# The adaLN scale's products placed ahead of block 0, decay matrices in three wide products, one weight split moved to VectorE

## The chip, the cores and the metric

The kernel runs on one core of a Trainium2 chip. Its time is the device time of one execution in microseconds (us). TensorE (PE) multiplies matrices, VectorE (DVE), ScalarE (ACT) and GpSimd (POOL) work on vectors, and SyncE (SP) issues all the transfers of this kernel. Each engine takes its instructions strictly in the order in which the program was written, and waits where an operand isn't ready, so one late operand holds everything behind it on that engine.

## The reference, cut to what matters

One layer of a hybrid backbone: 1024 latent and 128 context tokens of width 1024 pass an adaptive layer norm, one wide projection, differential attention and a retention scan in both directions, gates, an output projection and a last layer norm. The change touches the modulation at the start, and the table of decays of the retention.

```python
mod = silu(cond) @ w_mod + b_mod
shift, scale, gate = split(mod, 3)
h = layernorm(x) * (1 + scale) + shift
proj = h @ w_in                    # qa, ka, va, za, qr, kr, vr, zr
...
log_g = log1p(-exp2(ret_decay))    # (2, 8): one per direction and head
decay_in = where(rel >= 0, exp(log_g * max(rel, 0)), 0)   # 128 x 128, each head and direction
inner = (q @ k.T) * decay_in       # in chunks of 128 tokens
```

## The kernel before

Tokens and context stand together as nine tiles of 128 rows (1152 columns once they are turned over). A float32 operand of the large products is split into a high part in the matrix engine's short float format (`whi`, of ACT) and the remainder (`wlo`), and each product is done as three: high by high, high by low, low by high. All engines' instructions are written out by one Python program, which carries a plan of its own: `Sched` (L40) keeps an estimated time for each engine, several generators ("streams") yield the time at which they can go on, and whichever is due next writes its instructions. So a change of an estimated cost moves later instructions too.

**First stage, `phase_h` (L385).** For each of the nine tiles of x, DVE and ACT normalise, PE turns over eight 128x128 squares into two banks of PSUM of the pool `tp` (which has two banks), and ACT copies them to `xnT`. In between, PE works out the scale of the modulation with the condition vector as the stationary operand: `scale_k(g, k)` is one product of block k of the condition with rows of the weights `wk`; the group g = 0 gives scale and shift of the blocks 0 and 1, g = 1 the scale of the blocks 2 and 3 (256 columns wide), g = 2 that of the blocks 4 to 7 (512 columns wide). `scale_cols(g)` has ACT copy the two resulting rows out of PSUM (`rows`), PE turn them into columns, and DVE add the bias into `m1` (printed `m`) and `sh`. The shift of the blocks 2 to 7 comes from DVE alone (`by_rows`, two row products a block; `junk` in the trace). `mod(j)` then makes block j of `Y`: an affine form `hf` of `xnT` (DVE for block 0, ACT for the others), the high part (ACT), the low part (DVE). As soon as a block is there, `k_part` adds its products to six running sums, three column chunks for each of two jobs (`qr` and `kr`, the list `first`): part 0 is high by high, part 1 takes the weights' low part, part 2 the low part of `Y`. The last two blocks are done in `last_parts`.

**The stages behind it, `phase_a` (L611).** A stream `dense` (L328) runs one projection after the other: k of head 0, then the first V job of the retention (`vr`, nine row tiles of 256 columns), q of head 0, k of head 1, the first V of attention, and so on. It loads two jobs ahead, and splits the weights of a job (`Job.split`, L292) just before it writes the products of the job ahead of it; the low parts are POOL's, except for the first job. The results go through two banks of PSUM (`dn`), so a chunk can start only when the chunk two before it has been read out: for q and k by DVE's shuffle into `sw` and its product into `rt` (rotary embedding, finished by POOL), for `vr` by a copy on ACT. Beside that stream `core` (the retention) runs, which begins with `decays` (L725): a chain of small operations on DVE up to `kdec`, and then for each of eight heads two exponentials on ACT (`ef`, `eb`) and three products on DVE, which make `DT`, the 128x128 decay matrix of that head. `ef` has two buffers there, and `eb` one.

Of the kernel before, what the change touches and what calls it, by code (L numbers as in the profile page):

```python
# [11 lines left out]
F32 = mybir.dt.float32  # L12
F32R = mybir.dt.float32r
AF = mybir.ActivationFunctionType
ALU = mybir.AluOpType
# [3 lines left out]
P = 128  # L19
D = 1024  # L20
KT = D // P
NL = 1024
NT = NL + P
NTILE = NT // P
NH = 8
CW = 384
# [113 lines left out]
def hybrid_step(ctx: ExitStack, tc: tile.TileContext, I: dict, O: dict):  # L140
# [14 lines left out]
    def act(out, in_, func=AF.Copy, after=None, **kw):  # L155
        nc.scalar.activation(out, in_, func, **kw)  # L156
        extra = sum(not isinstance(v, (int, float)) for v in kw.values())
        return sch.op("act", 0.06 + out.free_size() / 1200 + 0.09 * extra, after)
# [4 lines left out]
    def v_tt(out, a, b, op, after=None):  # L163
        nc.vector.tensor_tensor(out, a, b, op=op)  # L164
        return sch.op("dve", 0.07 + out.free_size() / 960, after, in_sbuf(a, b))
# [56 lines left out]
    pz = ctx.enter_context(tc.tile_pool(name="pz", bufs=1))  # L222
# [13 lines left out]
    def psum_now(tag):  # L236
        t, tok = psum(tag)
        tok[0] = 0.0
        return t
# [15 lines left out]
    class Job:  # L255
        def __init__(self, kind, srcs, rhs, evac, gate=None, pool2=None, pre=None, need=None):
            self.kind, self.srcs, self.rhs, self.evac = kind, srcs, rhs, evac
            self.gate, self.pool2, self.pre = gate, pool2, pre
            self.raw, self.hi, self.lo = [], [], []
            self.ready = 0.0  # L260
            self.need = need

        def load(self):
            for s in self.srcs:
# [60 lines left out]
    def dense(nxt, mark):  # L325


        cur = nxt()  # L328
        cur.load()
        yield 0  # L330
        cur.split("v")
        ahead = nxt()
        ahead.load()
        yield 0
        while cur is not None:
            if ahead is not None:
                ahead.split()
            after = nxt() if ahead is not None else None
            if after is not None:
                after.load()  # L340
            if cur.gate is not None:
                yield cur.gate
            yield from cur.run()
            cur, ahead = ahead, after
        done[mark] = True
# [16 lines left out]
    def phase_h(first, load_decays, decays_y):  # L362

        es = ExitStack()
        p0 = es.enter_context(tc.tile_pool(name="p0", bufs=1, reuse_waits="tile"))
        with es:
# [27 lines left out]
            GS = ((0, 4), (0, 2), (2, 6))  # L394
# [58 lines left out]
            def scale_k(g, k):  # L453

                n = (GS[g][1] - GS[g][0]) * P
                if k == 0:
                    scale_ps[g] = psum_now("tp" if g else "dn")
                mm(scale_ps[g][0:2, :n], sc[:, k, :], wm[g, k], k == 0, k == KT - 1)

            def scale_cols(g):  # L460

                n = GS[g][1] - GS[g][0]
                rows = p0.tile([2, 512], F32, tag="rows", name="rows")
                act(rows[:, :n * P], scale_ps[g][0:2, :n * P])
                tp = psum_now("tp")
                for j in range(n):
                    nc.tensor.transpose(tp[:, 2 * j:2 * j + 2], rows[:, j * P:(j + 1) * P], ident[0:2, 0:2])
                    sch.t += 0.107
                for j0, dst, a, m, one in (((0, m1, 0, 2, 1.0), (2, sh, 0, 2, 0.0)), ((0, m1, 2, 2, 1.0),),
                                           ((0, m1, 4, 4, 1.0),))[g]:  # L470
                    c0 = 8 + a if one else a
                    v_stt(dst[:, a:a + m, :], tp[:, 2 * j0:2 * (j0 + m)].rearrange("p (j r) -> p j r", r=2), one,
                          bm[:, c0:c0 + m].rearrange("p (j o) -> p j o", o=1).to_broadcast([P, m, 2]),
                          ALU.add, ALU.add)
# [15 lines left out]
            for i in range(NTILE):  # L490
                if i + 2 < NTILE:
                    stats(i + 2)
                if i + 1 < NTILE:
                    normalise(i + 1)
                for g in range(2):
                    tp = psum_now("tp")
                    for k in range(4):
                        kk = g * 4 + k
                        tpose(tp[:, k * P:(k + 1) * P], xt[i][:, kk * P:(kk + 1) * P])
                    act(xnT[:, g * 4:(g + 1) * 4, i * P:(i + 1) * P],  # L500
                        tp.rearrange("p (k c) -> p k c", k=4))
                for k in ((), (0, 1), (2,), (3,), (4,), (5,), (6, 7), (), ())[i]:
                    scale_k(0, k)
                if i >= 6:
                    (lambda: first[0].split_hi(), lambda: scale_cols(0), lambda: None)[i - 6]()
                if i == 7:
                    first[1].split_hi()
                if i == 2:
                    first[0].load()
                    first[1].load()  # L510
                    load_shift(2)
                    load_wk(1, 0)
                    load_wk(1, 4)
                    load_shift(3)
                    for k in range(0, KT, 2):
                        load_wk(2, k)
# [33 lines left out]
                    load_decays()  # L550

            mod(0)
            acc = [[psum_now(("dn", "dn", "a", "a", "a", "a")[3 * n + c]) for c in range(NC)] for n in range(2)]
            vw = [j.views() for j in first]

# [11 lines left out]
            for k in range(KT - 2):  # L567
                mod(k + 1)
                for part in range(3):
                    for n in range(2):  # L570
                        k_part(n, k, part)
                        if (k, part, n) in ((0, 1, 0), (2, 0, 1)):
                            scale_cols(1 + k // 2)
                    if part == 0 and k < 2:
                        for q in range(KT):
                            scale_k(k + 1, q)
                if k == 2:
                    next(stream)
            mod(KT - 1)
# [31 lines left out]
    def phase_a():  # L611
# [113 lines left out]
        def decays():  # L725
# [34 lines left out]
            yield act(kdec, kdec, AF.Exp) + 1.3  # L760
            v_ts(kdec, kdec, 0.125, None, ALU.mult)
            act(g128, lg[:, 24:32], AF.Exp, scale=float(P))
            for h in range(NH):
                ef = pz.tile([P, CW], F32, tag="tz", name="ef", bufs=2)
                eb = pa.tile([P, P], F32, tag="ust", name="eb")
                act(ef[:, :P], cst[:, 0, :], AF.Exp, scale=lg[:, h:h + 1])
                yield act(eb[:, :P], cst[:, 1, :], AF.Exp, scale=lg[:, 8 + h:9 + h])
                v_tt(ef[:, :P], ef[:, :P], cst[:, 2, :], ALU.mult)
                v_tt(eb[:, :P], eb[:, :P], cst[:, 3, :], ALU.mult)
                v_tt(DT[:, h, :], ef[:, :P], eb[:, :P], ALU.add)  # L770

        def cache():
            ts = {}
# [170 lines left out]
        jobs = []  # L944
# [12 lines left out]
            return f  # L957

        jobs[-1].evac = last_evac
        todo.extend(jobs)  # L960
        dma(rc, I["rope_c"])
        dma(rsn, I["rope_s"])
# [698 lines left out]
```

## Time and profile before

| | |
|---|---|
| median of three timed runs | 1690.24 us (1687.55, 1690.24, 1691.09) |
| the profiled execution's own time | 1692.03 us |
| its span, first to last instruction | 1690.2 us |
| mean granted clock of TensorE | 0.994 |
| bytes moved | 237.36 MB, mean 140 GB/s |

The kernel is read as a line of TensorE work with gaps in it. In a row of the timeline the first column is the start in us, the second the length of the group, then engine, line, operation, written operand <- read operands, shapes and count; in square brackets stands how long the engine had been idle before it, and what ended that wait. Most operations are written by helpers, so a line number says little: L149 is every product, L153 every transpose, L156 every operation of ACT, L164 and L185 the two-operand products of DVE and POOL, L169 and L173 DVE's operations with scalars. In a table of windows PEclk is the clock that TensorE was granted in that stretch, as a share of full speed.

### The profile page before, as it was taken

The page shows a single profiled execution, that of the slowest core. Times are in us where ns is not written, and L with a number is a line of the kernel's source. Part 1 is how long each engine was busy: PE and PEld are TensorE (multiplying, and loading weights), DVE is VectorE, ACT ScalarE, POOL GpSimd, SP SyncE. Part 2 cuts the span into 40 slices and gives each one's busy share as a digit, 9 for nine tenths or more (in the row PEclk, how much of TensorE's full clock was granted, in tenths as well). Part 3 has the DMA queues.
Part 4 walks back from the last instruction along what each step waited for, and adds up shares of the span by engine and source line. Part 5 has one row for each costly group of instructions (what it writes and reads, how often), then busy time and mean ns, then how long its engine had stood idle before and what let it go on. Part 6 is the DMA issues. An engine that isn't in the chain of part 4 may idle for free.

```text
span 1690.2 us, 27057 instructions
## 1 busy us (share of the span) xinstructions
PE 1657.3 (98%) x10515; PEld 1610.2 (95%) x10515; DVE 853.6 (51%) x1679; ACT 606.1 (36%) x1136; POOL 784.4 (46%) x546
## 2 busy tenths in 40 slices
PE   7999999999999999999999999999999999999998
PEld 4799999999999999999999999999999999999886
DVE  7736407314605536656565666566656033134666
ACT  5532222221221245455455555545555220012200
POOL 2246227334725657654757475757655321112200
PEclk9999999999999999999999999999999999999999
DMA  8254303421321383534434343525252577854532
GB/s 332 94 149 127 123 27 114 128 93 45 104 102 44 125 267 111 189 106 133 139 116 146 113 155 110 162 92 168 74 160 87 208 263 262 264 180 131 159 125 87
DMA packets 135697, 237.36 MB, mean 140 GB/s; under 512 B 15801, under 2 KB 103313, under 8 KB 134545
## 3 DMA queue, kind: packets, MB, share of 16 engines
q1 hardware_dynamic: 135568, 235.63, 43.3%
q8 instruction: 83, 1.36, 0.3%
q14 instruction: 46, 0.37, 0.1%
HBM read 161.08 MB, written 74.49 MB: 139 GB/s over the span
## 4 chain that ended last, share of the span: by engine, by line
PE 89%; DVE 3%; issue 2%; ACT 2%; DMA 1%; POOL 1%; SPq 0%; DVEq 0%; POOLq 0%; ACTq 0%
PE dn L149 59%; PE S L149 8%; PE o L149 6%; PE e L149 6%; PE a L149 5%; PE tp L153 5%; PE tp L149 1%; ACT E L156 1%; DMA xt<-in_x 1%; DMA ORd<-goh 0%; DVE eps L173 0%; DVE r L173 0%; DVE E L173 0%; ACT whi L156 0%; DVE nm L1097 0%
## 5 line engine op out<-in xcount | busy, mean ns | idle before, releaser
L149 PE MATMUL dn<-Y,whi 128*128 128x384 f32 x3200 | 829.7, 340 | 3.3 <-DVE rt L164 2.2
L149 PEld LDWEIGHTS dn<-Y,whi 128*128 128x128 f32 x3200 | 567.4, 189 | 4.9 <-DVE rt L164 2.5
L149 PE MATMUL dn<-Y,wlo 128*128 128x384 f32 x1600 | 535.6, 336 | 0.0
L185 POOL TENSOR_TENSOR wlo<-raw,whi 128x1024 fp32r<-128x1024 f32 x85 | 204.7, 2412 | 412.5 <-ACT whi L156 403.1
L149 PEld LDWEIGHTS dn<-Y,wlo 128*128 128x128 f32 x1600 | 300.5, 188 | 1.4 <-issue 0.9
L1097 DVE TENSOR_REDUCE nm<-S 128x1 f32<-128x1152 f32 x144 | 178.1, 1237 | 174.2 <-PE S L149 173.9
L189 POOL TENSOR_SCALAR E<-E,r 128x640 f32<-128x640 f32 x64 | 143.6, 2243 | 127.5 <-DVE r L173 87.0
L156 ACT ACTIVATE E<-S,nm 128x1152 f32<-128x1152 f32 x144 | 162.3, 1127 | 79.4 <-DVE nm L1097 74.5
L149 PE MATMUL dn<-whi,Y 128*128 128x256 f32 x864 | 158.9, 284 | 2.4 <-ACT vr L156 1.9
L149 PEld LDWEIGHTS dn<-whi,Y 128*128 128x128 f32 x864 | 135.4, 191 | 2.8 <-ACT vr L156 2.1
L149 PE MATMUL o<-wTh,V 128*128 128x256 f32 x576 | 133.5, 290 | 0.0
L156 ACT ACTIVATE wTh<-tp 128x512 fp32r<-128x512 f32 (+1 forms) x168 | 88.6, 543 | 112.9 <-PE tp L153 109.2
L156 ACT ACTIVATE whi<-raw 128x1024 fp32r<-128x1024 f32 x88 | 92.2, 1054 | 91.2 <-PE dn L149 85.0
L149 PE MATMUL dn<-wlo,Y 128*128 128x256 f32 x432 | 122.1, 283 | 0.0
L164 DVE TENSOR_TENSOR wTl<-tp,wTh 128x512 fp32r<-128x512 f32 (+1 forms) x168 | 99.6, 612 | 24.0 <-ACT wTh L156 24.0
L185 POOL TENSOR_TENSOR E<-E 128x640 f32<-128x640 f32 x64 | 100.4, 1569 | 5.3
L149 PE MATMUL S<-K,QH 128*128 128x384 f32 (+1 forms) x400 | 94.4, 339 | 6.2 <-ACT E L156 6.2
L149 PEld LDWEIGHTS o<-wTh,V 128*128 128x128 f32 x576 | 99.4, 188 | 0.2
L149 PE MATMUL S<-K,QL 128*128 128x384 f32 (+1 forms) x400 | 92.6, 335 | 0.0
L173 DVE SCALAR_TENSOR_TENSOR gt<-gt,dn 128x384 f32<-128x384 f32 x48 | 26.6, 554 | 120.2 <-DMA gt<-Gd 59.6
L153 PE MATMUL tp<-ident,E 128*128 128x128 f32 x584 | 86.8, 272 | 0.0
L169 DVE TENSOR_SCALAR KD<-tp,kdec 128x256 f32<-128x256 f32 (+1 forms) x48 | 16.0, 407 | 138.1 <-PE tp L153 138.1
(203 smaller groups left out, 2476.5 us busy)
## 6 DMA issues: line engine op xcount, KB each, us to landing
K<-Kd SPq DMA_DIRECT2D x8, 1280.0 KB, 8.3
Gd<-gt SPq DMA_DIRECT2D x48, 192.0 KB, 2.5
V<-Vd SPq DMA_DIRECT2D x24, 384.0 KB, 4.9
gt<-Gd SPq DMA_DIRECT2D x48, 192.0 KB, 2.5
Y<-OAd SPq DMA_DIRECT2D x16, 576.0 KB, 3.9
raw<-in_w_gate SPq DMA_DIRECT2D x16, 512.0 KB, 3.6
QH<-Qh SPq DMA_DIRECT2D x64, 128.0 KB, 3.0
QL<-Ql SPq DMA_DIRECT2D x64, 128.0 KB, 2.8
```

The lines of the kernel that those rows point to most:

```text
L149: nc.tensor.matmul(out, lhsT=lhsT, rhs=rhs, start=start, stop=stop)
L153: nc.tensor.transpose(out, in_, ident)
L156: nc.scalar.activation(out, in_, func, **kw)
L164: nc.vector.tensor_tensor(out, a, b, op=op)
L169: nc.vector.tensor_scalar(out, a, s1, s2, op0=op0, **kw)
L173: nc.vector.scalar_tensor_tensor(out, a, s, b, op0=op0, op1=op1, **kw)
L185: nc.gpsimd.tensor_tensor(out, a, b, op=op)
L189: nc.gpsimd.tensor_scalar(out, a, s1, None, op0=op0)
L1097: nc.vector.tensor_reduce(nm[:, m:m + 1], ps[:, :nb, :kw], axis=AX.XY, op=ALU.max, negate=True)
```

## The change

There are three edits. The scale's group 1 is no longer written after the first products of block 0: its first four products stand between the turning of tile 8 and block 0, the other four after block 0's part 0, and the copy of its rows follows at once; group 2 keeps its place after block 1's part 0, but the copy of its rows is written there instead of at the transposes. The copy of the rows is a function of its own, `scale_rows`; for group 0 it moves up by one tile, and the splitting of the first job's weights (`whi`) moves down by one tile for that. In `decays` the exponentials of the eight heads go into two tiles of 128x1024 each, and DVE makes all eight matrices in three products. The low parts of the first `vr` job are given to DVE.

```diff
@@ Job.__init__ / dense
             self.need = need
+            self.low = "p"
...
-                ahead.split()
+                ahead.split(ahead.low)
@@ phase_h
+            rows_of = {}
+
+            def scale_rows(g):
+                n = GS[g][1] - GS[g][0]
+                rows_of[g] = p0.tile([2, 512], F32, tag="rows", name="rows")
+                act(rows_of[g][:, :n * P], scale_ps[g][0:2, :n * P])
+
             def scale_cols(g):
                 n = GS[g][1] - GS[g][0]
-                rows = p0.tile([2, 512], F32, tag="rows", name="rows")
-                act(rows[:, :n * P], scale_ps[g][0:2, :n * P])
+                rows = rows_of[g]
...
-                if i >= 6:
-                    (lambda: first[0].split_hi(), lambda: scale_cols(0), lambda: None)[i - 6]()
+                if i == 6:
+                    scale_rows(0)
                 if i == 7:
+                    first[0].split_hi()
+                    scale_cols(0)
                     first[1].split_hi()
...
             mod(0)
+            for q in range(4):
+                scale_k(1, q)
...
                         k_part(n, k, part)
-                        if (k, part, n) in ((0, 1, 0), (2, 0, 1)):
+                        if (k, part, n) == (0, 0, 1):
+                            for q in range(4, KT):
+                                scale_k(1, q)
+                            scale_rows(1)
+                        if (k, part, n) in ((0, 1, 1), (2, 0, 1)):
                             scale_cols(1 + k // 2)
-                    if part == 0 and k < 2:
+                    if (k, part) == (1, 0):
                         for q in range(KT):
-                            scale_k(k + 1, q)
+                            scale_k(2, q)
+                        scale_rows(2)
@@ decays
+            ef = pa.tile([P, NH, P], F32, tag="SS", name="ef")
+            eb = pa.tile([P, NL], F32, tag="QD", name="eb").rearrange("p (h i) -> p h i", i=P)
             for h in range(NH):
-                ef = pz.tile([P, CW], F32, tag="tz", name="ef", bufs=2)
-                eb = pa.tile([P, P], F32, tag="ust", name="eb")
-                act(ef[:, :P], cst[:, 0, :], AF.Exp, scale=lg[:, h:h + 1])
-                yield act(eb[:, :P], cst[:, 1, :], AF.Exp, scale=lg[:, 8 + h:9 + h])
-                v_tt(ef[:, :P], ef[:, :P], cst[:, 2, :], ALU.mult)
-                v_tt(eb[:, :P], eb[:, :P], cst[:, 3, :], ALU.mult)
-                v_tt(DT[:, h, :], ef[:, :P], eb[:, :P], ALU.add)
+                act(ef[:, h, :], cst[:, 0, :], AF.Exp, scale=lg[:, h:h + 1])
+                f = act(eb[:, h, :], cst[:, 1, :], AF.Exp, scale=lg[:, 8 + h:9 + h])
+                yield f
+            v_tt(ef, ef, cst[:, 2:3, :].to_broadcast([P, NH, P]), ALU.mult)
+            yield v_tt(eb, eb, cst[:, 3:4, :].to_broadcast([P, NH, P]), ALU.mult)
+            yield v_tt(DT, ef, eb, ALU.add)
@@ phase_a
+        jobs[0].low = "v"
```

On TensorE, at the end of the first stage's transposes (tile 8 is the row with `raw`, `tp<-wk,sc` is group 1, `dn<-Y` and `a<-Y` are the running sums), the order moves like this:

```order
 L153 MATMUL tp<-ident,raw 128x128 x8
+L149 MATMUL tp<-wk,sc 2x256 x4
 L149 MATMUL dn<-Y,whi 128x384 x2
 L149 MATMUL a<-Y,whi 128x384 x4
-L149 MATMUL tp<-wk,sc 2x256 x8
+L149 MATMUL tp<-wk,sc 2x256 x4
 L149 MATMUL dn<-Y,wlo 128x384 x2
-L149 MATMUL a<-Y,wlo 128x384
-L467 MATMUL tp<-ident,rows 128x2 x2
-L149 MATMUL a<-Y,wlo 128x384 x3
+L149 MATMUL a<-Y,wlo 128x384 x4
+L474 MATMUL tp<-ident,rows 128x2 x2
```

Half of group 1 now stands ahead of block 0's first product, and the two transposes of its rows stand behind all six products of part 1.

On ScalarE, at the same place (the first four copies are those of the tiles 5 and 6, then come tile 7, tile 8 and the three pieces of block 0's high part):

```order
 L156 ACTIVATE xnT<-tp 128x4x128 x4
-L156 ACTIVATE whi<-raw 128x1024
+L156 ACTIVATE rows<-dn 2x512
 L156 ACTIVATE xnT<-tp 128x4x128 x2
-L156 ACTIVATE rows<-dn 2x512
-L156 ACTIVATE whi<-raw 128x1024
+L156 ACTIVATE whi<-raw 128x1024 x2
 L156 ACTIVATE xnT<-tp 128x4x128 x2
 L156 ACTIVATE Y<-hf 128x384 x3
```

The copy of group 0's rows and the first high split have changed places. Further down on ScalarE the copy of group 2's rows moves from behind block 3's pieces to ahead of them.

On VectorE, in the stage behind it (`kdec` ends the chain of small operations; the shuffle into `sw` and the product into `rt` read out the first chunk of k of head 0):

```order
 L164 TENSOR_TENSOR kdec<-kx,lg 128x16
-L666 STREAM_SHUFFLE sw<-dn 128x384
+L164 TENSOR_TENSOR wlo<-raw,whi 128x1024 x2
+L682 STREAM_SHUFFLE sw<-dn 128x384
 L164 TENSOR_TENSOR rt<-dn,rc 128x384
```

The two low splits of `vr`, which were the first work of POOL after its two memsets, now stand between `kdec` and that shuffle. The three wide products stand behind the shuffle and product of k's last chunk, where the 24 products of 128x128 stood, and the next work of DVE after them is the shuffle of q's first chunk, in both orders. ScalarE's exponentials keep their place, but the copy of the last chunk's context part (`rt<-dn 128x128`) stands behind two pairs of them and one high part of k (`qkh`), where it stood ahead of all pairs. Beyond this, the planner puts the retention's work of head 0 some products later into the stream of projections; from the retention of head 1 on the order of all engines is that of before.

## The prediction

> **What bounds the kernel now.** I read the page first, then TensorE's timeline for its gaps, the windows for its clock, and at each gap the timelines of the engines that it waited for.
>
> ```profile
> PE 1657.3 (98%) x10515; PEld 1610.2 (95%) x10515; DVE 853.6 (51%) x1679; ACT 606.1 (36%) x1136; POOL 784.4 (46%) x546
> ```
>
> TensorE is busy for 1657 of 1690.2 us. The edits neither add nor remove a product, so only TensorE's gaps, and the time in which it ran at a lower clock, can be won. Two stretches of a lower clock stand in the stages that the change touches; these are windows of 2 us, the last of 20 (length, then busy time of PE, weight load, DVE, ACT, POOL; then the granted clock, DMA share, GB/s):
>
> ```profile
> 32.00:34.00 2.00, 1.46 (x5) 1.13 (x4) 2.00 (x3) 1.87 (x3) 0.00 (x0) 0.69 1.07 394
> 34.00:36.00 2.00, 2.00 (x7) 0.53 (x6) 1.97 (x4) 1.34 (x2) 0.00 (x0) 0.50 0.60 230
> 36.00:38.00 2.00, 2.00 (x11) 0.76 (x10) 1.96 (x4) 0.00 (x0) 0.00 (x0) 0.96 0.05 18
> ...
> 92.00:94.00 2.00, 0.38 (x3) 0.38 (x4) 1.67 (x6) 0.98 (x4) 0.38 (x1) 1.00 0.00 0
> 94.00:96.00 2.00, 2.00 (x13) 2.00 (x12) 1.64 (x4) 2.00 (x6) 1.00 (x1) 0.55 0.05 12
> 96.00:98.00 2.00, 2.00 (x13) 2.00 (x13) 1.58 (x7) 0.97 (x4) 0.00 (x0) 0.60 0.96 210
> ...
> 100.00:120.00 20.00, 20.00 (x158) 20.00 (x157) 1.04 (x5) 5.60 (x10) 4.78 (x2) 1.00 0.52 128
> ```
>
> If the clock is either full or half, 0.55 and 0.60 make (0.45 + 0.40) x 2 / 0.5 = 3.4 us of half clock, which loses 1.7 us of work, right behind a gap of TensorE at 92 to 94. The first three rows hold 1.2 + 2.0 + 0.2, the same 3.4 us, also behind gaps.
>
> **Part 1, the first stage.** Here is TensorE from tile 8 to the products of group 2, and ACT beside it:
>
> ```profile
> 29.07 1.11 PE L153 MATMUL tp<-ident,raw 128*128 128x128 f32 x8
> 31.31 0.85 PE L149 MATMUL dn<-Y,whi 128*128 128x384 f32 x2 [1.13 <-ACT Y L156]
> 32.71 1.64 PE L149 MATMUL a<-Y,whi 128*128 128x384 f32 x4 [0.55 <-ACT Y L156]
> 34.28 4.53 PE L149 MATMUL tp<-wk,sc 128*2 128x256 f32 x16
> 38.74 0.62 PE L149 MATMUL dn<-Y,wlo 128*128 128x384 f32 x2
> ...
> 42.49 7.03 PE L149 MATMUL tp<-wk,sc 128*2 128x512 f32 x16
> ```
>
> ```profile
> 25.24 1.05 ACT L156 ACTIVATE whi<-raw 128x1024 fp32r<-128x1024 f32 x1
> 27.14 1.09 ACT L156 ACTIVATE xnT<-tp 128x512 f32<-128x512 f32 x2 [0.85 <-PE tp L153]
> 28.11 0.57 ACT L156 ACTIVATE rows<-dn 2x512 f32<-2x512 f32 x1
> ...
> 29.76 1.09 ACT L156 ACTIVATE xnT<-tp 128x512 f32<-128x512 f32 x2
> 30.73 0.94 ACT L156 ACTIVATE Y<-hf 128x384 fp32r<-128x384 f32 x2
> 32.13 0.52 ACT L156 ACTIVATE Y<-hf 128x384 fp32r<-128x384 f32 x1 [0.46 <-DVE hf L169]
> ```
>
> TensorE waits 1.13 + 0.55 us for block 0's high part. In ACT's new order the rows' copy (0.5) goes into the idle 0.85 ahead of 27.14, and both splits (1.0 each) follow tile 7 at 28.1. Tile 8's copies then run from 30.1 to 31.1 instead of 29.76 to 30.85, and the three high pieces from 31.1 to 32.5: DVE has `hf` ready earlier, as group 0's rows are copied ahead of 27.14 instead of at 28.11, so ACT's wait of 0.46 goes. The last piece ends at 32.5 against 32.65.
>
> TensorE can't start group 1 at once: both banks of `tp` hold tile 8, and the first is free when half of its copies are done, at 30.6. From there, four products. A product of group 2 (512 columns) counts as two in the trace, at 7.03 / 16 = 0.44 us each and full clock, so one of 256 columns takes 2 x 0.22, and four take 1.8. That gives 30.65 + 1.8 = 32.5, when block 0 is ready. A product of 384 columns takes 0.17 (two last 0.51 with the 0.34 of one, in rows below), so six of block 0 bring it to 33.55, four more of group 1 35.35. From the end of group 1 to the start of group 2 the trace has 42.49 - 38.74 = 3.75 us, which stays: **group 2 starts at 39.1 instead of 42.49, 3.4 us earlier.** Of these, 1.7 are the half clock. If the clock drops again, 1.7 are left. The gap that remains reaches from tile 8's last transpose (28.2, when tile 7 is copied, and 1.1 for the eight: 29.3) to 30.65, 1.3 us; before there were 1.13 and 0.55. Less idle time at that place speaks for the full clock.
>
> What hid group 1 before was nothing; what could come last now is the chain behind group 2, as its rows' copy stands ahead of block 3 on ACT:
>
> ```profile
> 49.55 0.59 ACT L156 ACTIVATE rows<-tp 2x512 f32<-2x512 f32 x1 [2.81 <-PE tp L149]
> 53.21 0.17 DVE L173 SCALAR_TENSOR_TENSOR m<-tp,bm 128x8 f32<-128x8 f32 x1 [3.86 <-PE tp L467]
> 64.34 0.21 ACT L156 ACTIVATE dec<-dec 128x32 f32<-128x32 f32 x1
> 64.47 1.36 DVE L164 TENSOR_TENSOR Y<-hf,Y 128x1152 fp32r<-128x1152 f32 x1 [1.40 <-ACT Y L156]
> 67.26 0.51 PE L149 MATMUL dn<-Y,whi 128*128 128x384 f32 x2
> ```
>
> From `m` to `dec` ACT makes four blocks in 11.0 us, 2.73 each. Block 7's low part ends at 65.83 and is used at 67.26: 1.43 us to spare. In the new order (on the old clock of TensorE, group 2 ending at 49.55) come rows 0.5, block 3 in 2.73, its low part 1.36, and then `m`: 54.3 instead of 53.2. That eats 1.1 of the 1.43, so 0.3 is left; I cost it at nothing. Without that cover it costs up to 1.1. Weights and shift loads come no later: the DMA share falls to 0.60 and then 0.05 in the windows above, so group 2's weights had landed by 36, and the next shift loads wait for group 1's buffers, which come free earlier.
>
> **Part 2, k of head 0 and the low parts of vr.**
>
> ```profile
> 69.84 1.23 DVE L164 TENSOR_TENSOR wlo<-raw,whi 128x1024 fp32r<-128x1024 f32 x1 [0.19 <-ACT whi L156]
> 74.63 4.78 POOL L185 TENSOR_TENSOR wlo<-raw,whi 128x1024 fp32r<-128x1024 f32 x2 [9.12 <-DVE tmp L169]
> 74.82 2.27 DVE L169 TENSOR_SCALAR tmp<-tmp 128x32 f32<-128x32 f32 x1
> 77.12 2.33 DVE L164 TENSOR_TENSOR tmp<-tmp 128x32 f32<-128x32 f32 x1
> 79.49 0.18 DVE L169 TENSOR_SCALAR tmp<-tmp 128x32 f32<-128x32 f32 x1
> 81.01 0.54 DVE L164 TENSOR_TENSOR rt<-dn,rc 128x384 f32<-128x384 f32 x1
> 79.05 0.34 PE L149 MATMUL dn<-Y,wlo 128*128 128x384 f32 x1
> 81.61 0.62 PE L149 MATMUL dn<-Y,whi 128*128 128x384 f32 x2 [2.22 <-DVE rt L164]
> ```
>
> Two operations of DVE on 128x32, whose like take 0.18 us, last 2.27 and 2.33, and each ends with one of POOL's two low splits (half way, at 77.0, and at 79.4). The whole chain, and behind it the first shuffle and `rt`, is late by 4.2 us, and TensorE has no free bank: 2.4 us lost (81.61 against 79.05 + 0.17). With both splits on DVE (two at a pitch of 1.15, out of the 1.23 of the first row: 2.3 us, right behind the chain) `rt` ends at 81.55 - 4.2 + 2.3 = 79.65, and TensorE goes on at 79.7, 0.5 us late instead of 2.4. **Gain 1.9 us**, bounded by 2.4 above and by -2.3 below (the splits add and the chain doesn't shrink). I take a value near the upper end, as POOL's ends and DVE's agree within 0.1 us, and POOL has nothing else queued in that stretch until the first rotary product.
>
> **Part 3, the decay matrices.**
>
> ```profile
> 85.91 0.28 PE L149 MATMUL dn<-whi,Y 128*128 128x256 f32 x1
> 88.97 2.41 POOL L185 TENSOR_TENSOR wlo<-raw,whi 128x1024 fp32r<-128x1024 f32 x1 [0.34 <-ACT whi L156]
> 89.31 2.22 DVE L164 TENSOR_TENSOR ef<-ef,cst 128x128 f32<-128x128 f32 x1 [1.47 <-ACT ef L156]
> 92.90 0.40 ACT L156 ACTIVATE eb<-cst,lg 128x128 f32<-128x128 f32 x1 [2.62 <-DVE DT L164]
> 93.62 0.39 PE L149 MATMUL dn<-whi,Y 128*128 128x256 f32 x1 [1.85 <-ACT vr L156]
> 112.59 0.38 ACT L156 ACTIVATE vr<-dn 128x256 f32<-128x256 f32 x1 [1.53 <-PE dn L149]
> 115.45 0.38 ACT L156 ACTIVATE vr<-dn 128x256 f32<-128x256 f32 x1 [2.48 <-PE dn L149]
> ```
>
> DVE's first `ef` product again lasts as long as POOL's split. ACT's second `eb` waits 2.62 us for the only buffer, and `vr`'s copy behind it keeps TensorE waiting. One tile of `vr` takes 2.86 us (115.45 - 112.59), nine take 25.7; from 85.91 to 115.4 are 29.5. **The 3.75 us too many are the gain**: 2.0 of the gap and 1.7 of half clock behind it. With two wide tiles no exponential waits for DVE. The three products (about 1.2 us each by the split's row, 3.7 in all, up to 7.4 if POOL's work collides) stand before DVE's next duty, the shuffle of q, which comes after the whole of `vr`; nobody waits. Wherever the cover of `vr` is gone, they would cost those 3.7.
>
> **The sum.** 3.4 + 1.9 + 3.75 = 9.05 us. Against the profiled execution: 1692.03 - 9.05 = **1683.0 us**. The median before is 1.8 below that execution, and the runs spread over 3.5, about two half-clock stretches. I read this as executions in which one such stretch fell out, and don't take the 1.8 off again; the low end of the range does. What lies behind (the retention of head 0 moved within the stream, SP's loads of its state moved past two stores of q) I cost at nothing: TensorE is busy for all of 100 to 120 us, with the planner's same rules behind it, and the order is the old one again after that.
>
> **Rivals.**
>
> [...] *The half clock is chance.* If a stall of 1.85 us doesn't set it, and where it falls is luck of each execution, only 9.05 - 2 x 1.7 = 5.65 is won: 1686.4. For it: the spread of the runs. Against it: both stretches begin right behind a gap. [...]
>
> *One cover fails.* The remaining gap of 1.3 us draws the half clock again, or ACT's chain behind group 2 ends last: 1.7 or up to 1.1 less, at most 1684.7.
>
> *DVE's chain isn't slowed by POOL.* Then the splits only add 2.3 us ahead of the first shuffle: 3.4 + 3.75 - 2.3 = 4.85, 1687.2. Against it: the matching ends.
>
> *Slower: ACT's queue.* The copy of the last chunk's context part stands behind two pairs of exponentials and a `qkh` that waits for POOL. Its bank is needed after the first tile of `vr`, 85.91 - 1.9 + 2.86 = 86.9; DVE's part of it (a shuffle and a product, together 1 us behind 84.0) ends at about 85.0, and the copy itself takes 0.3, so there are 1.6 us to spare. Beyond them every us of waiting (for POOL, or for the tile `cst`) is one of TensorE, with 1.7 for the clock. To lose all the gain and 3.4 us more, ACT must stand 12.4 us; a hold of 15 gives 1692.03 - 9.05 + 13.4 + 1.7 = 1698.1. Nothing in the trace holds it that long.
>
> *It doesn't do what it says*: the gain comes back as new gaps in the retention of head 0, whose work moved: about 1690.
>
> **How the numbers follow.** Forecast 0.48; one cover fails 0.22; clock by chance 0.14; chain not slowed 0.08; slower 0.04; given back 0.04. What a measurement can tell from no change is about 0.2%, 3.4 us, so faster means below 1686.9: 0.48 + 0.22 + 0.14 = 0.84. Within it: 0.08 + 0.04 = 0.12. Slower: 0.04. The range takes in the first three: up to 1686.6, and down by the 1.8 and the two small gaps that I left (1.3 and 0.5): 1679.4.
>
> **What would show it.** Right: the row of 16 products of 512 columns starts near 39, no window under 0.9 in 30 to 40 us or around 85 to 95, no gap over 0.5 before the third chunk of k, `vr` copies 2.86 apart from the first to the last, and DVE's small operations all near 0.2. Wrong: a clock under 0.7 near 33, a row of block 7's products that waits for DVE's `Y`, or a `vr` product that waits for ACT.

## The result, and the profile after

| | before | after |
|---|---|---|
| median of four timed runs | 1690.02 us (1687.55 to 1691.09) | 1680.66 us (1679.17 to 1683.20) |
| the profiled execution's own time, and its span | 1692.03, 1690.2 us | 1680.30, 1678.5 us |
| TensorE's mean granted clock | 0.994 | 0.998 |

The ratio of the medians is 0.9948, with a 95% interval of 0.9931 to 0.9965: faster by 0.5%, and 1680.66 lies 2.3 us below the forecast, inside its range. The two profiled executions are 11.7 us apart, the medians 9.4. From the page of the changed kernel, the busy time of the engines:

```profile
PE 1652.8 (98%) x10515; PEld 1606.1 (96%) x10515; DVE 846.0 (50%) x1660; ACT 605.7 (36%) x1136; POOL 780.1 (46%) x544
```

TensorE has the same 10515 products and 4.5 us less busy time, although none was taken away. The row counts how long products took, and at half clock they take longer: in the run with seven gaps (below) the products of 128x256 follow each other after 0.21 us at half clock and 0.12 at full. The changed kernel has three stretches of half clock fewer (counted below), and one costs 1.4 to 1.6 us where the runs below single it out, so the clock accounts for about all of the 4.5 us. The rest of the 11.7 us is idle time of TensorE that is gone.

**First stage.** TensorE in the changed kernel from tile 8 (`raw`) to group 2, then ACT beside it, in the timeline's columns:

```profile
28.00 1.09 PE L153 MATMUL tp<-ident,raw 128*128 128x128 f32 x8
30.37 1.89 PE L149 MATMUL tp<-wk,sc 128*2 128x256 f32 x8 [1.28 <-ACT xnT L156]
32.19 0.62 PE L149 MATMUL dn<-Y,whi 128*128 128x384 f32 x2
...
33.43 1.89 PE L149 MATMUL tp<-wk,sc 128*2 128x256 f32 x8
...
39.02 7.03 PE L149 MATMUL tp<-wk,sc 128*2 128x512 f32 x16
```

```profile
27.83 2.00 ACT L156 ACTIVATE whi<-raw 128x1024 fp32r<-128x1024 f32 x2
29.72 1.08 ACT L156 ACTIVATE xnT<-tp 128x512 f32<-128x512 f32 x2
30.68 1.36 ACT L156 ACTIVATE Y<-hf 128x384 fp32r<-128x384 f32 x3
```

One gap of 1.28 us is left where there were 1.13 and 0.55; it ends when half of tile 8's copies are done, which stand behind the two splits on ACT. Group 1 takes 1.89 + 1.89 us instead of 4.53, because the clock stays full (granted 1.00 in all windows of 2 us from 30 to 38, where before had 0.50 from 34 to 36). Group 2 starts at 39.02 instead of 42.49. About 0.4 us of that is the execution's start: TensorE waited 3.5 us for its first operand, and before 4.0, and a tile that neither kernel treats differently is turned over at 20.28 instead of 20.71.

**k of head 0 and `vr`.** DVE from the end of the small chain to the first chunk's read-out, and TensorE beside it:

```profile
71.35 0.18 DVE L169 TENSOR_SCALAR tmp<-tmp 128x32 f32<-128x32 f32 x1
...
72.74 2.36 DVE L164 TENSOR_TENSOR wlo<-raw,whi 128x1024 fp32r<-128x1024 f32 x2
...
75.64 0.54 DVE L164 TENSOR_TENSOR rt<-dn,rc 128x384 f32<-128x384 f32 x1
```

```profile
75.59 0.34 PE L149 MATMUL dn<-Y,wlo 128*128 128x384 f32 x1
76.23 0.62 PE L149 MATMUL dn<-Y,whi 128*128 128x384 f32 x2 [0.30 <-DVE rt L164]
...
80.50 0.28 PE L149 MATMUL dn<-whi,Y 128*128 128x256 f32 x1
```

Every small operation takes 0.2 us now, the two splits 2.36, and TensorE waits 0.30 us (0.47 between the end of the work and the next start) where it waited 2.22. In windows of 40 us (PE's busy time is the first number, the granted clock the third from the end), two of before and two of after:

```profile
0.00:40.00 40.00, 31.48 (x153) 18.75 (x154) 28.01 (x56) 23.67 (x37) 9.44 (x24) 0.96 0.89 330
...
80.00:120.00 40.00, 36.54 (x268) 36.34 (x269) 14.99 (x42) 14.46 (x36) 16.31 (x15) 0.96 0.42 103
```

```profile
0.00:40.00 40.00, 33.12 (x169) 20.62 (x170) 29.23 (x59) 23.57 (x37) 9.45 (x24) 1.00 0.96 356
...
80.00:120.00 40.00, 40.00 (x302) 39.97 (x301) 9.53 (x17) 13.27 (x33) 19.28 (x15) 1.00 0.58 158
```

In the changed kernel TensorE has no idle time at all from 80 to 120 us, against 3.46 us, and both stretches run at full clock.

**Where the 11.7 us arise**, by the same instruction in both traces: group 2 starts 3.47 us earlier, `vr` 5.41 (85.91 against 80.50), its last copy 9.03 (115.45 against 106.42), the first score product of attention 9.7, the last 10.2, the last product of all 11.7. So 9.03 us have been won when `vr` ends; the other 2.7 arise behind it.

### The profile page after: what moved, and what is told of

Same layout as the page of the kernel before. It is cut to its first block, busy times and chain, and to the rows that moved or that the text cites. A ratio compares the mean times of both kernels' runs of the same rounds, so it can differ in the third digit from the quotient of the medians.

```text
span 1678.5 us, 27038 instructions
## 1 busy us (share of the span) xinstructions
PE 1652.8 (98%) x10515; PEld 1606.1 (96%) x10515; DVE 846.0 (50%) x1660; ACT 605.7 (36%) x1136; POOL 780.1 (46%) x544
## 4 chain that ended last, share of the span: by engine, by line
PE 86%; issue 4%; DVE 3%; DMA 3%; POOL 2%; ACT 2%; SPq 1%; DVEq 0%; POOLq 0%; ACTq 0%
PE dn L149 55%; PE S L149 8%; PE o L149 6%; PE e L149 6%; PE a L149 5%; PE tp L153 5%; PE tp L149 1%; DMA gt<-Gd 1%; ACT E L156 1%; SPq L203 1%; DMA xt<-in_x 1%; DVE eps L173 0%; DMA ORd<-goh 0%; DVE r L173 0%; DVE E L173 0%
## 5 line engine op out<-in xcount | busy, mean ns | idle before, releaser
L185 POOL TENSOR_TENSOR wlo<-raw,whi 128x1024 fp32r<-128x1024 f32 x83 | 199.9, 2411 | 394.7 <-ACT whi L156 388.4
```

Of the source, the lines that this page charges most:

```text
L185: nc.gpsimd.tensor_tensor(out, a, b, op=op)
```

## The experiments

A profile gives four marks for each kernel, which don't depend on what happens later: the start of group 2; the time from the start of k of head 0 to that of `vr`; the time from there to the start of `vr`'s last copy; and the number of stretches at half clock, each about 3.4 us long, up to the last products.

| kernel | group 2 at | k to `vr` | `vr` | half clocks | own time of the profiled execution |
|---|---|---|---|---|---|
| before | 42.49 | 15.01 | 29.54 | 4 | 1692.03 |
| the change | 39.02 | 13.07 | 25.92 | 1 | 1680.30 |
| first edit alone | 38.95 | 16.44 | 27.42 | 1 | 1685.09 |
| second alone | 42.49 | 15.02 | 25.92 | 3 | 1691.18 |
| third alone | 43.00 | 13.06 | 26.39 | 1 | 1685.93 |
| without the third | 39.04 | 16.57 | 25.92 | 1 | 1685.01 |
| without the second | 38.95 | 13.06 | 26.39 | 2 | 1686.40 |

### Each edit alone

The theory: the three gains are independent, and each stands at its own place. The rival: two of them are one and the same wait.

```diff
# first edit alone, on the kernel before: everything of the diff in phase_h, nothing else
# second alone: only this, in decays
+            ef = pa.tile([P, NH, P], F32, tag="SS", name="ef")
+            eb = pa.tile([P, NL], F32, tag="QD", name="eb").rearrange("p (h i) -> p h i", i=P)
...
+            v_tt(ef, ef, cst[:, 2:3, :].to_broadcast([P, NH, P]), ALU.mult)
# third alone: only this
+        jobs[0].low = "v"
```

> The kernel before with only the first edit (the scale's products and the copies of its rows). If the sum's terms stand by themselves: group 2's 16 rows start near 39.1 us instead of 42.49 (39.0 in the changed kernel), no half clock near 33 us; k of head 0 to the first product of vr stays at 15.0 us (70.90 to 85.91 before), vr from its first product to its last copy stays at 29.5. If the half clock behind block 0 is chance, group 2 starts at 40.8 or so in about half of such executions, with a window near 0.5.

> The kernel before with only the decays' wide products. If they account for all of part 3: vr takes 25.8 to 25.9 us from its first product to its last copy instead of 29.5, with no gap and no half clock, while the stage from k of head 0 to vr stays at 15.0 with its gap of 2.2 and the two long operations of DVE, as POOL still makes vr's low parts; group 2 starts at 42.5 (or 40.8 without the half clock, if that is chance). If instead POOL's work is what keeps the copies waiting, vr stays over 27.

> The kernel before with only vr's low parts on VectorE. If POOL's two splits stretch DVE's chain: the small operations all take about 0.2 us, k of head 0 to vr takes 13.1 us instead of 15.0, and the gap before k's third chunk is 0.3 to 0.5. If the long operations have another cause, the splits add 2.3 us in front of the first shuffle and the stage takes 17.3. vr stays near 29.5 in both (its wait for the decays is untouched), with the half clock behind its gap if a gap sets it; if that is chance, 27.8.

The first edit moves group 2 by 3.5 us and leaves the gap before the third chunk of k, as expected; that gap now drew half clock, which it had not before (16.44 instead of 15.01). The expectation that `vr` stays at 29.5 was wrong: it took 27.42, since its gap shrank from 1.85 to 1.25 us and no half clock followed it. The second takes all of `vr`'s excess away, 29.54 to 25.92, and leaves k as it was, DVE's two long operations included. The third does what was expected of k, 15.01 to 13.06, and then something that was not: `vr` falls to 26.39 by itself. TensorE's waits from 60 to 118 us, in the kernel with the third edit alone (engine, what waited and for what; us in total, times, longest):

```profile
PE dn L149 <- DVE rt L164: 0.3, 1, 0.3
PE dn L149 <- ACT vr L156: 0.2, 1, 0.2
```

Of the wait of 1.85 us for `vr`'s copy, 0.2 is left. What else moved stands in that kernel's DVE rows:

```profile
83.08 0.75 DVE L164 TENSOR_TENSOR ef<-ef,cst 128x128 f32<-128x128 f32 x1 [0.27 <-ACT ef L156]
...
88.95 2.09 DVE L164 TENSOR_TENSOR ef<-ef,cst 128x128 f32<-128x128 f32 x1 [0.32 <-ACT ef L156]
```

The first head's product starts at 83.08, 1.4 us ahead of `vr` (which starts at 84.5 in this kernel), where before it started 3.4 us behind it (89.31 against 85.91). The product that lasts 2 us, as long as a split on POOL, is now a later head's. So fewer exponentials are left when `vr`'s copies come. The first edit alone shows the same in small, in the row of DVE's first product and the row of TensorE that ends `vr`'s gap:

```profile
86.59 2.21 DVE L164 TENSOR_TENSOR ef<-ef,cst 128x128 f32<-128x128 f32 x1 [1.19 <-ACT ef L156]
90.91 0.38 PE L149 MATMUL dn<-whi,Y 128*128 128x256 f32 x1 [1.25 <-ACT vr L156]
```

There the product starts 2.79 us behind `vr` (at 83.80) instead of 3.40, 0.61 earlier, and the gap is 0.60 us shorter. That the earlier start shortens the wait fits these three kernels, but wasn't tried by itself.

### The change without one edit

```diff
# without the third
-        jobs[0].low = "v"
# without the second: decays as in the kernel before
```

> The changed kernel with vr's low parts back on POOL. If this edit is what cures the chain in front of the first shuffle: two operations of DVE last 2.3 us again, a gap of 2.2 returns before k's third chunk, and k of head 0 to vr takes 15.0 us (16.4 if that gap draws half clock) instead of 13.1; vr stays at 25.9, as the wide decays cover it. If the wide decays have cured both, 13.1 stays.

> The changed kernel with the decays head by head as before. By the prediction's third term vr goes back from 25.9 to 29.5 us (27.8 without half clock). By the run with only the low parts moved, which took 26.4, the second and the third edit hide the same wait, and vr comes out at 26.4 here too: then the third term is right in size, but most of it would have come with the low parts alone. k of head 0 to vr stays at 13.1.

Without the third edit DVE's two long operations are back to the hundredth, beside the two splits of POOL, and k of head 0 to `vr` takes 16.57 us, since the gap of 2.21 us is back and half clock follows it; DVE's rows and POOL's of that kernel:

```profile
71.37 2.27 DVE L169 TENSOR_SCALAR tmp<-tmp 128x32 f32<-128x32 f32 x1
73.67 2.33 DVE L164 TENSOR_TENSOR tmp<-tmp 128x32 f32<-128x32 f32 x1
```

```profile
71.18 4.77 POOL L185 TENSOR_TENSOR wlo<-raw,whi 128x1024 fp32r<-128x1024 f32 x2 [8.17 <-DVE tmp L169]
```

That settles the cause in part 2: the two operations are long in all four kernels of the table in which POOL's splits run beside them, and take 0.18 and 0.19 us in the three in which they don't. The second ends at 76.00 here, where POOL's splits end at 75.95. A scalar operation is held up (2.27 us) as one with two operands is (2.33).

Without the second edit `vr` takes 26.39 instead of 25.92. So beside the third edit the second is worth 0.47 us in `vr`, and beside the second the third is worth nothing there: each hides the same wait, and 3.15 of the 3.62 us come with either. About 1.5 of these are the half clock behind that wait, and it stays away with the first edit alone too.

The table's last column doesn't add up from these marks. One reason is the half clocks that fall behind `vr`; the other is that the four kernels that have the second or the third edit, but not all three, have idle time of TensorE there, where the changed kernel and the one before have almost none. TensorE's wait from 120 to 200 us with the second edit alone:

```profile
PE tp L153 <- DVE KD L169: 2.0, 1, 2.0
```

And in the change without the second edit:

```profile
PE a L149 <- DVE inn L164: 1.3, 1, 1.3
PE tp L153 <- ACT on L156: 0.5, 1, 0.5
```

The planner places the retention of head 0 by estimated times, so each mixture of the edits gets another order there. Between 120 and 200 us TensorE is idle for 0.5 us in the kernel before, 0.1 in the changed one, and 1.8 to 2.9 in these four. The prediction's "given back" rival, new gaps in the retention of head 0, came true in them and not in the changed one. Beside the third edit, then, the second is worth 0.47 us in `vr` and 1.7 more in the retention.

### What draws half clock

The prediction put 1.7 + 1.7 us on the clock, on the reading that the gaps ahead of the two half clocks draw them. In the trace of before, half clock begins at 32.74, 94.18, 722.23 and 1435.62 us, which lie 18, 184 and 209 times 3.413 us apart, and in the stretch of that length ahead of each TensorE was busy for 51%, 46%, 43% and 41%. The limits that the expectations below set on a gap, in us, are the author's estimates. The rival was chance. To try it, gaps were made: extra copies on ACT, overwritten by the tile's own copy, hold up seven copies of `vr`.

```diff
+ HOLD = {(0, 6): 13, (1, 2): 11, (1, 6): 14, ...}
+                for _ in range(HOLD.get((p, i), 0)):
+                    nc.scalar.activation(R["vr", p][:, i, 0:P], ident, AF.Copy)
```

> The changed kernel with 10 to 17 extra copies of 128 columns on ScalarE ahead of the copy of one vr tile at seven places (they write a part of the tile that the copy behind them overwrites), each 0.3 us. TensorE then waits at each: 0.30 x copies - 2.45 us by the trace's 2.86 a tile, so about 0.6, 0.9, 1.2, 1.5, 1.8, 2.1 and 2.7. If a gap sets the half clock by the busy share of a stretch of 3.4 us, the gaps of 2.1 and 2.7 are followed by 3.4 us of half clock, those under 1.2 never, and 1.5 to 1.8 depending on where they lie; every half-clock stretch starts a whole number of 3.41 us from every other. [...]

A miss: the copies wait for nothing, so ACT did them in its idle time ahead of the tile, and only one gap came about, of 0.85 us. The second form reads the tile's own bank, so that the copies start when the products are done (up to three copies more at a place):

```diff
-                    nc.scalar.activation(R["vr", p][:, i, 0:P], ident, AF.Copy)
+                    nc.scalar.activation(R["vr", p][:, i, 0:P], ps[:, 0:P], AF.Copy)
```

> The changed kernel with 11 to 18 extra copies of 128 columns on ScalarE at seven vr tiles, now reading that tile's own bank, so that they start only when TensorE is done with it (in the run before they started up to 2.5 us early and hid in ScalarE's idle time). About 0.31 us each less 2.45: gaps of 1.0 to 3.1 us where nothing else stands between the tiles, less where the retention's products do. If a half-clock stretch follows when TensorE was busy for less than about half of a stretch of 3.41 us on a fixed grid, gaps over 1.9 are always followed by one, gaps under 1.0 never, and in between the grid decides; all stretches lie whole multiples of 3.41 us apart. [...]

Seven gaps of 1.01 to 3.17 us came about. The three longest, as the row of TensorE that ends each:

```profile
242.64 0.39 PE L150 MATMUL dn<-whi,Y 128*128 128x256 f32 x1 [2.24 <-ACT vr L157]
...
382.00 0.39 PE L150 MATMUL dn<-whi,Y 128*128 128x256 f32 x1 [3.17 <-ACT vr L157]
...
506.29 0.39 PE L150 MATMUL dn<-whi,Y 128*128 128x256 f32 x1 [2.55 <-ACT vr L157]
```

Half clock followed the gaps of 2.24 and 2.55 us, from 243.93 and from 506.75, and neither the longest nor the four others. Between the two starts lie 262.82 us, 77 times 3.413. Cut into stretches of that length, counted from there, the execution reads so (windows of one stretch each: length, PE's busy time, weight load, DVE, ACT, POOL; then the granted clock):

```profile
240.52:243.93 3.41, 1.29 (x11) 1.29 (x12) 0.00 (x0) 2.16 (x8) 0.00 (x0) 1.00 0.00 0
243.93:247.34 3.41, 3.41 (x18) 3.41 (x17) 0.00 (x0) 0.20 (x1) 0.00 (x0) 0.50 0.00 0
...
377.05:380.46 3.41, 1.79 (x16) 1.58 (x14) 0.00 (x0) 3.06 (x12) 0.00 (x0) 1.00 0.00 0
380.46:383.88 3.42, 1.88 (x15) 1.88 (x16) 0.00 (x0) 1.64 (x6) 0.00 (x0) 1.00 0.00 0
383.88:387.29 3.41, 3.41 (x31) 3.41 (x30) 0.00 (x0) 0.38 (x1) 0.00 (x0) 1.00 0.02 5
...
503.34:506.75 3.41, 0.86 (x7) 0.66 (x6) 0.00 (x0) 2.89 (x11) 0.00 (x0) 1.00 0.00 0
506.75:510.16 3.41, 3.41 (x19) 3.41 (x17) 0.00 (x0) 0.00 (x0) 0.00 (x0) 0.50 0.00 0
```

A stretch in which TensorE was busy for 38% or 25% is followed by exactly one stretch of half clock. The gap of 3.17 us lay across a border: 52% and 55% on the two sides, and nothing followed. So the expectation that every gap over 1.9 us is followed was wrong twice, for this one and for one of 1.93 us (ended at 105.57), which lay across a border too; the busy share of the stretch held. The same in the kernel before, in stretches counted from its own half clocks:

```profile
77.11:80.53 3.42, 2.28 (x14) 1.96 (x12) 3.17 (x7) 0.00 (x0) 2.30 (x1) 1.00 0.00 0
80.53:83.94 3.41, 2.33 (x13) 2.33 (x14) 3.27 (x9) 0.82 (x3) 2.58 (x5) 1.00 0.00 0
...
90.77:94.18 3.41, 1.56 (x13) 1.36 (x12) 3.07 (x7) 1.16 (x4) 1.61 (x2) 1.00 0.20 80
94.18:97.60 3.42, 3.42 (x18) 3.42 (x17) 2.72 (x8) 2.54 (x8) 1.00 (x1) 0.50 0.49 108
```

The gap of 1.85 us lay inside one stretch (46% busy) and drew half clock; that of 2.22 us lay across two (67% and 68%) and didn't. With the first edit alone the same gap (2.21 us) came 3.5 us earlier and fell inside one (42% busy):

```profile
74.43:77.84 3.41, 1.44 (x9) 1.12 (x7) 3.17 (x9) 0.00 (x0) 1.62 (x2) 1.00 0.00 0
77.84:81.26 3.42, 3.18 (x10) 3.18 (x11) 2.42 (x8) 0.83 (x3) 3.26 (x6) 0.50 0.00 0
```

### Is the first stage's half clock luck?

All eight products ahead of block 0 instead of four is the same work in another order, and would show whether four is the point of the edit.

```diff
             mod(0)
-            for q in range(4):
+            for q in range(KT):
                 scale_k(1, q)
+            scale_rows(1)
...
-                        if (k, part, n) == (0, 0, 1):
-                            for q in range(4, KT):
-                                scale_k(1, q)
-                            scale_rows(1)
```

> The changed kernel with all eight products of group 1 ahead of block 0 instead of four. In the changed kernel's trace TensorE runs without a gap from 30.4 us to beyond group 2, so only the order of the same work moves: group 2 starts at 39.0 as before. If the four behind block 0's part 0 were covering something (block 0's high pieces or the low parts), or if block 0 had been ready only later than TensorE reached it, the start would move by up to 0.9 us one way or the other.

Group 2 starts at 40.38. The gap in front of group 1 is the same 1.29 us, and this time half clock follows; the stretch with most of the gap (59% busy; the one with that gap in the changed kernel is 62%) and the one behind it:

```profile
26.83:30.24 3.41, 2.00 (x17) 1.43 (x15) 2.11 (x5) 3.41 (x6) 0.00 (x0) 1.00 1.05 388
30.24:33.66 3.42, 3.22 (x8) 0.98 (x9) 3.35 (x6) 1.87 (x5) 0.00 (x0) 0.50 1.06 389
```

That costs 1.4 us of group 1 (5.19 us instead of twice 1.89), which is all by which group 2 is late: eight ahead or four is the same. And the gap that the change leaves can draw half clock. It did so in one of the nine traces that have a gap of this size there (this one; not in the changed kernel, nor in the others with the new first stage); with the old first stage all three traces had it.

### Taking the gap away, and the order on ACT

The gap is there because two splits of 1.0 us stand on ACT ahead of tile 8's copies. So the second split goes behind them, and six products ahead of block 0:

```diff
                 if i == 7:
                     first[0].split_hi()
                     scale_cols(0)
+                if i == 8:
                     first[1].split_hi()
...
-            for q in range(4):
+            for q in range(6):
                 scale_k(1, q)
```

> The changed kernel with two lines moved: the second high split follows tile 8's copies on ScalarE instead of standing ahead of them, and six products of group 1 (not four) stand ahead of block 0. Tile 8's copies run 0.9 us earlier, so the bank for group 1 is free at 29.4 instead of 30.3, the gap of 1.28 shrinks to about 0.3, six products end at 32.2 when block 0's last high piece ends, and group 2 starts at 38.0 instead of 39.0; no half clock there. Total 1.0 us less than the changed kernel's (0.06%), which the timed runs can hardly show, so the start of group 2 decides. If ScalarE's block 0 pieces are what bounds the stage, the gap only moves behind the six products and group 2 stays at 39.0.

The changed kernel with ACT's order of before (first split, then tile 7's copies, then the rows):

```diff
                 if i == 6:
-                    scale_rows(0)
-                if i == 7:
                     first[0].split_hi()
+                if i == 7:
+                    scale_rows(0)
                     scale_cols(0)
                     first[1].split_hi()
```

> The changed kernel with ScalarE's order of before around tile 7 (first split, then tile 7, then the rows' copy), the products of group 1 as changed. By the prediction's reading the products need no change on ScalarE, which only makes the first pieces wait less: block 0's last piece ends at about 32.4 instead of 32.0, the first four products start up to 0.3 us earlier, and group 2 starts at 39.0 to 39.4. If the rows' earlier copy is what makes the edit work, group 2 starts at 40 or later.

The change once more with nothing altered, beside both on one chip:

> The changed kernel itself, timed beside the run with two lines moved and the kernel before on the same chip: 0.993 to 0.997 of before, as in the first comparison; group 2 at 39.0, with half clock near 33 us or without.

| kernel | median | runs | ratio to before (its median there 1689.75, 11 runs) |
|---|---|---|---|
| second split behind tile 8 | 1679.50 us (1677.72 to 1681.85) | 6 | 0.9939 (0.9920 to 0.9959) |
| the change again | 1682.08 us (1678.35 to 1683.82) | 6 | 0.9951 (0.9931 to 0.9970) |
| ACT's old order | 1679.81 us | 1 | |

With the second split behind tile 8, TensorE's rows:

```profile
28.07 1.09 PE L153 MATMUL tp<-ident,raw 128*128 128x128 f32 x8
29.50 2.75 PE L149 MATMUL tp<-wk,sc 128*2 128x256 f32 x12 [0.34 <-ACT xnT L156]
...
38.15 7.03 PE L149 MATMUL tp<-wk,sc 128*2 128x512 f32 x16
```

The gap falls from 1.28 to 0.34 us. From tile 8's first transpose to group 2 it takes 10.08 us, and in the changed kernel 11.02: 0.94 us won, in the trace. The medians, 1679.50 and 1682.08, lie the same way round, but the runs overlap, so they don't show it. ACT's order of before gives 12.75 us from tile 7's transposes to group 2 (26.54 to 39.29), and the changed kernel run again 12.87 (26.58 to 39.45), so that part of the change is worth 0.1 us at most, whatever its sign. ACT's wait for `hf`, which the new order takes away, is back with the old one:

```profile
32.23 0.53 ACT L156 ACTIVATE Y<-hf 128x384 fp32r<-128x384 f32 x1 [0.46 <-DVE hf L169]
```

This second run of the changed kernel also shows how far luck reaches. Its profiled execution has nearly the same idle time as the first (9.7 us from 120 to 1640 us, and 10.9), no half clock at all, and a span of 1676.6 us; the first had one half clock and 1678.5. Here is a place, in the untouched part, where the one had it and the other not (TensorE's row that ends the gap, first in the first execution, then in the second):

```profile
676.71 0.33 PE L149 MATMUL S<-K,QH 128*128 128x128 f32 x1 [1.23 <-ACT E L156]
```

```profile
677.45 0.33 PE L149 MATMUL S<-K,QH 128*128 128x128 f32 x1 [1.23 <-ACT E L156]
```

The first is followed by half clock at 677.6, the second isn't. Against the grid the first wait lies inside one stretch (64% busy), and the second across a border at 676.75 (84% and 79%). The kernel before had its two late half clocks, at 722 and 1436, behind waits of 2.50 and 2.01 us in parts that the change doesn't touch either.

## Why the prediction was right

The forecast was 1692.03 - 9.05 = 1683.0. By the end of `vr` the two traces are 9.03 us apart, or 8.6 without the earlier start.

**Part 1: 3.4 predicted, 3.47 measured**, 3.05 without the earlier start. The path is the predicted one: tile 8's half copy, four products, block 0, four products. ACT's new order does what the prediction says, it takes away the wait of 0.46 us for `hf`, but TensorE gains nothing by it: the old order has that wait and gives the same time within 0.1 us. What helps is that TensorE has four products to do before it needs block 0. The half clock's 1.7 us was counted as gone since "less idle time at that place speaks for the full clock". It was gone, but not for certain: a gap of 1.28 us drew it in one of nine traces. And 1.7 us for a stretch is a little too much here and in part 3: it takes every product to need twice the time, and where the runs single a stretch out it costs 1.41 us (eight products ahead), 1.43 (first edit alone, 16.44 - 15.01) and 1.56 (without the third, 16.57 - 15.01).

**Part 2: 1.9 predicted, 1.94 measured** (15.01 - 13.07). The cause, POOL's splits beside DVE's chain, is shown by taking the third edit out and by putting it in alone. The rival that DVE's chain isn't slowed by POOL has fallen.

**Part 3: 3.75 predicted, 3.62 measured** (29.54 - 25.92), with the copies at the predicted 2.86 us from the second on, and no wait for ACT left. The step "the 3.75 us too many are the gain" was right for the sum and gave the whole to the second edit: 3.15 us of it come with the third edit alone, by the order of the rows since the exponentials then start earlier. The half clock in it hangs on where the gap lies as well: with the first edit alone a gap of 1.25 us at that place drew none. Had the parts been asked for one by one, the answers would have been wrong: the third edit alone wins 1.95 + 3.15 in these two stages, the second alone 3.62, and the two together 5.56.

**What lies behind: costed at nothing, measured +0.4 us** (0.46 - 0.11) of idle time won between 120 and 200 us. It was right for this kernel, but the ground given, that TensorE is busy there and the planner's rules are the same, didn't carry it: under the same rules the other mixtures of the edits lose 1.3 to 2.4 us more there than the kernel before.

**The remaining 2.7 us** between the traces, which no term of the sum has: 0.7 up to the first score product (the 0.4 above in it); 0.5 up to the last, a part in which each execution had one half clock; and 1.5 behind it, where the one before had a half clock at 1436 and the one after had none. The rival "half clock is chance" is half right: it takes a gap, but whether a gap of 1.2 to 3.2 us draws it depends on where it lies against a grid of 3.413 us, and that grid lay elsewhere in the second execution of the same kernel (the border at 676.75 us instead of 677.60). The medians, over four executions each, are 9.36 apart, nearer the 9.05 of the sum; that the traces had won 9.03 by the end of `vr` is in part luck, since 0.4 of it is the earlier start.

The slower rival, ACT's queue, did not come about: the copy of k's last chunk (the 128x128 `rt<-dn` on ACT) stood at 82.33 and no product waited for it.

## What to carry to other kernels

Count a low clock behind a gap as a term of its own (1.4 to 1.6 us here, twice in the touched stages), and as one that the gap left by the change can still draw. When two edits relieve the same queue, run each alone before giving a gain to one of them: here 3.15 of 3.62 us belonged to either. Where a planner writes the order, a partial edit is another program, and its total says little; compare marks in the trace at the end of the stage that was touched.

## What the runs showed of the hardware

- Up to the last products, half clock came in stretches of 3.413 us on a grid that ran through the whole execution: in each of the thirteen traces every change of the clock lies a whole number of 3.413 us from the others. The two executions of the changed kernel had the grid at different places: the clock first rises at 8.59 and 7.74 us, with the first product at 3.45 and 3.57.
- On that grid, from 20 us to the last product, 14 stretches had TensorE busy for 46% or less, and every one was followed by one stretch of half clock (behind four of them no product was left). From 48% to 64% it went either way (nine were, 44 weren't), and above that none was. So in that range the busy share of a stretch didn't decide it alone. Of one wait, 1.23 us ahead of a score product, 18 lie inside one stretch, all 64% busy: the five that begin at 35% to 46% of the stretch were followed by half clock, the 13 that begin earlier than 24% or from 59% on were not. Other waits don't follow that (the changed kernel run again waits 1.28 us in its first stage from 38% of a stretch on, 60% busy, without half clock), so what else decides stays open.
- A DVE operation of 0.18 us took 2.27 us beside a two-operand operation of POOL (its splits of 128x1024, 4.77 us for two). That DVE loses time beside POOL could be read from the profile before; that moving the two splits also wins 3.15 us at another place could not.
